# A transformer block whose planner leaves GpSimd only the norms' inverse roots, with fixed buffers and a new plan

## The chip, the core and the metric

The kernel runs on one core of one Trainium2 chip. The metric is the time of one launch in microseconds of device time, taken as the median of several runs. Lower is better.

## What is computed

Two layers of a diffusion transformer block work on 512 latent tokens and 256 context tokens of width 1024, all in float32. In each layer three token mixers read the same normalised and modulated input and their outputs are joined before one output projection; then follows a gated feed-forward network (FFN).

```
for l in range(2):
    u  = modulate(rmsnorm(h),  shift, scale)   @ w_in[l]     # latent tokens
    uc = modulate(rmsnorm(hc), cshift, cscale) @ w_in[l]     # context tokens
    na  = neighborhood_attention(q, k, v, k_ctx, v_ctx, rpb) # 6 heads of 64, windows of 8 x 16
    mla = latent_attention(...)                              # 6 heads, low-rank q and kv, rope
    lru = gelu(lg) * (scan_forward + scan_backward)          # gated linear recurrence
    h  = h + g_m * (concat(na, mla, lru) @ w_out[l])
    h  = h + g_f * (silu(y @ w_gate) * (y @ w_up)) @ w_down,  y = modulate(rmsnorm(h))
    # the context tokens go the same way in layer 0 alone
```

The shifts, scales and gates come from a product of a condition vector with `ada_w` (1024 x 6144 for each layer).

## The kernel before, in words

Activations lie transposed: 128 channels on the partitions, tokens along the free dimension (768 in layer 0, 512 for most of layer 1). Each float32 matrix product runs on TensorE as three products of a high and a low part: `split` (a copy to the type fp32r for the high part, tile `whi` for weights and `s` for operands, then a subtraction for the low part, `wlo` or `s`). So each weight tile that comes by DMA (tile `wst`) costs a cast and a subtraction of 128 x 1024 on some engine before TensorE can use it. The FFN's two first products use Strassen's scheme of seven products for 2 x 2 blocks: sums and differences of weight blocks (`weights`, written into `wst`) and of the operand's blocks (`operands`, tiles `lo`, `tmp`, `s`), then sums of the products (`Side.all`, `together`).

A norm's inverse root is made in `rstd`: a few columns of sums of squares go through TensorE, are scaled on VectorE into a tile `rn` (line 561), raised to the power -0.5 on GpSimd (line 697, "a root" below), and spread over the tokens by transposes on TensorE (line 524).

No engine order is written by hand. Every operation is recorded as an `Op` with a cost for each engine that could run it (`t` TensorE, `v` VectorE, `s` ScalarE, `g` GpSimd, `d` DMA issue). `Order.place` is a list planner: it takes the operation that can start first by its own model of the clocks, ranks and buffers, puts it on the engine that it thinks best, and gives out the program in that order. The roots name GpSimd alone; copies, casts, sums, differences and memsets name two or three engines, so the planner chose GpSimd for 276 of them. Its model holds one more thing: VectorE operations that are marked `both` (no operand in PSUM) and GpSimd operations exclude each other on a port. An operation on one side that would start while the other side is busy was moved to that one's end when candidates were compared.

The order in which the mixer's steps are recorded, and a lead for each in rank, stand in a table of text (`PLAN`, `LEAD`), one list for each layer. Steps are named by what they do (`lru_*`, `latent_*`, `near_*`, `out_part k` for the split of the k-th operand of the output projection). The output projection itself (tiles `A<-s,whi` at a mixer's end) and the FFN are recorded after them, and the planner may place their instructions among the last steps.

Tiles of one tag share a number of buffers (`BUFS`, for instance 15 of `s`, 4 each of `wst`, `whi` and `wlo`). The planner's model took the buffer that came free first; the framework then picked which one in fact.

## Time and profile before

| | us |
|---|---|
| three runs | 1832.73, 1825.57, 1832.43 (median 1832.43) |
| the profiled execution, its own time | 1837.95 |
| span of the profiled execution | 1835.4 |
| TensorE (PE) busy | 1720.5 |
| VectorE (DVE) busy | 1340.2 |
| ScalarE (ACT) busy | 770.2 |
| GpSimd (POOL) busy | 407.5 |

PE is the time of matmuls, PEld that of weight loads beside them. The mean granted clock of TensorE is 0.975 of full speed. The stages by the trace: start to 46 us; mixer of layer 0 with its output projection to about 506; change to the FFN (norm, `operands`) to 552; FFN of layer 0 to 1058; the norm between the layers to 1104; mixer of layer 1 to 1426; its change to the FFN to 1518; FFN of layer 1 to the end. In the views an instruction is given by the line of its helper: L518 a matmul, L524 a transpose, L544 and L546 a copy or cast on ACT and on DVE, L548 the same on POOL, L554 a sum or difference on DVE or POOL, L588 a multiply-add on DVE, L697 a root.

### The profile page before, as it was taken

What the parts mean: (1) busy time and instruction counts of PE and PEld (TensorE: products, weight loads), DVE (VectorE), ACT (ScalarE), POOL (GpSimd) and SP (SyncE); (2) the same over time, 40 slices, a digit from 0 to 9 for tenths busy, and PEclk for the clock granted to TensorE, in tenths of its full rate; (3) what the DMA queues carried; (4) which work ended last, traced back from release to release, by engine and by line L of the source; (5) the groups of instructions that cost most, each with busy time, mean ns of one, the idle gap of its engine ahead of it and who ended that gap; (6) DMA issues with size and microseconds to landing.
All of it is one profiled execution on the core that took longest, in us unless ns stands there. A gap on an engine that the chain in (4) does not pass through costs nothing.

```text
span 1835.4 us, 27989 instructions
## 1 busy us (share of the span) xinstructions
PE 1720.5 (94%) x10616; PEld 1472.5 (80%) x10616; DVE 1340.2 (73%) x2361; ACT 770.2 (42%) x1382; POOL 407.5 (22%) x326
## 2 busy tenths in 40 slices
PE   8989999999979999999999989998889989999998
PEld 4877665767959898989899968776678788898897
DVE  6574356766498888877879677576686797788776
ACT  5282245664153343323223233744565343343343
POOL 0142133233072121210111022213243240001010
PEclk9999899999989999999999989999999989999999
DMA  8121123233012334243434141212011123323332
GB/s 336 58 74 62 39 69 104 78 116 127 29 35 90 105 98 129 81 141 112 151 125 138 61 142 47 65 58 72 24 38 30 35 65 108 104 93 98 98 104 92
DMA packets 90998, 166.66 MB, mean 91 GB/s; under 512 B 10480, under 2 KB 53872, under 8 KB 90864
## 3 DMA queue, kind: packets, MB, share of 16 engines
q1 hardware_dynamic: 90864, 164.88, 28.1%
q8 instruction: 83, 1.36, 0.3%
q14 instruction: 51, 0.42, 0.1%
HBM read 160.65 MB, written 4.19 MB: 90 GB/s over the span
## 4 chain that ended last, share of the span: by engine, by line
PE 64%; DVE 22%; DMA 5%; issue 4%; ACT 3%; POOL 2%; SPq 0%; DVEq 0%; ACTq 0%; POOLq 0%
PE A L518 36%; PE B L518 22%; DVE wlo L554 6%; PE B L524 5%; DVE tmp L554 3%; DMA ast<-in_ada_dram 3%; DVE s L554 3%; DVE wst L554 2%; DMA wst<-in_wg_dram 1%; DVE acc L588 1%; POOL rn L697 1%; DVE s L546 1%; DVE lo L588 1%; DVE lo L554 1%; DVE hr L588 1%
## 5 line engine op out<-in xcount | busy, mean ns | idle before, releaser
L518 PE MATMUL A<-s,whi 128*128 128x256 f32 (+2 forms) x2192 | 546.9, 341 | 17.6 <-ACT s L544 5.5
L518 PE MATMUL B<-s,whi 128*128 128x384 f32 (+2 forms) x2032 | 465.9, 323 | 17.8 <-ACT hr L544 4.3
L518 PEld LDWEIGHTS A<-s,whi 128*128 128x128 f32 x2192 | 375.5, 190 | 72.2 <-ACT s L544 7.4
L544 ACT CAST whi<-wst 128x1024 fp32r<-128x1024 f32 (+2 forms) x281 | 227.0, 817 | 439.9 <-PE A L518 225.8
L518 PEld LDWEIGHTS B<-s,whi 128*128 128x128 f32 x2032 | 347.6, 193 | 32.2 <-ACT hr L544 4.6
L518 PE MATMUL A<-s,wlo 128*128 128x256 f32 (+2 forms) x1064 | 345.7, 338 | 1.2 <-DVE wlo L554 1.2
L554 DVE TENSOR_TENSOR wlo<-wst,whi 128x1024 fp32r<-128x1024 f32 (+3 forms) x303 | 319.9, 1066 | 12.1 <-ACT whi L544 8.4
L518 PE MATMUL B<-s,wlo 128*128 128x384 f32 (+2 forms) x1016 | 301.9, 320 | 0.2 <-DVE wlo L554 0.2
L518 PE MATMUL A<-lo,whi 128*128 128x512 f32 (+1 forms) x776 | 216.7, 358 | 4.7 <-DVE hr L588 1.8
L518 PEld LDWEIGHTS A<-s,wlo 128*128 128x128 f32 x1064 | 197.4, 191 | 15.8 <-DVE wlo L554 2.0
L518 PEld LDWEIGHTS B<-s,wlo 128*128 128x128 f32 x1016 | 190.6, 193 | 3.4 <-DVE wlo L554 0.5
L697 POOL TENSOR_TENSOR rn<-rn,con 128x12 f32<-128x12 f32 (+5 forms) x44 | 84.6, 1925 | 445.0 <-DVE rn L561 437.8
L518 PEld LDWEIGHTS A<-lo,whi 128*128 128x128 f32 x776 | 136.6, 188 | 31.7 <-issue 3.3
L588 DVE SCALAR_TENSOR_TENSOR hr<-A,mod,hr 128x512 f32<-128x512 f32 (+1 forms) x153 | 100.6, 659 | 60.2 <-PE A L518 60.1
L554 POOL TENSOR_TENSOR wst<-wst,wst 128x512 f32<-128x512 f32 x35 | 54.3, 1553 | 371.2 <-DVE wst L554 328.1
L518 PE MATMUL A<-lo,wlo 128*128 128x512 f32 (+1 forms) x388 | 136.2, 356 | 0.0
L518 PE MATMUL A<-s,s 128*128 128x512 f32 (+1 forms) x508 | 120.5, 354 | 14.2 <-ACT lo L533 4.5
L518 PEld LDWEIGHTS A<-s,s 128*128 128x128 f32 x508 | 81.2, 194 | 36.5 <-ACT lo L533 10.1
L546 DVE CAST whi<-wst 128x1024 fp32r<-128x1024 f32 (+3 forms) x45 | 32.7, 727 | 101.1 <-PE A L518 82.0
L588 DVE SCALAR_TENSOR_TENSOR acc<-ast,cc,acc 128x256 f32<-128x256 f32 x168 | 88.5, 527 | 19.2 <-DMA ast<-in_ada_dram 17.8
L554 POOL TENSOR_TENSOR wlo<-wst,whi 128x512 fp32r<-128x512 f32 (+3 forms) x25 | 40.9, 1637 | 262.2 <-ACT whi L544 260.9
L518 PE MATMUL B<-s,s 128*64 128x256 f32 (+2 forms) x720 | 87.5, 347 | 0.7 <-DVE sm L1411 0.5
(206 smaller groups left out, 2371.4 us busy)
## 6 DMA issues: line engine op xcount, KB each, us to landing
ast<-in_ada_dram SPq DMA_DIRECT2D x320, 128.0 KB, 2.2
wst<-in_wg_dram SPq DMA_DIRECT2D x44, 512.0 KB, 3.5
wst<-in_wu_dram SPq DMA_DIRECT2D x44, 512.0 KB, 3.5
wst<-in_wd_dram SPq DMA_DIRECT2D x80, 256.0 KB, 2.7
wst<-in_win_dram SPq DMA_DIRECT2D x32, 512.0 KB, 3.7
wst<-in_wout_dram SPq DMA_DIRECT2D x16, 512.0 KB, 3.7
hr<-in_x_dram SPq DMA_DIRECT2D x16, 384.0 KB, 3.6
s<-in_ada_dram SPq DMA_DIRECT2D x8, 768.0 KB, 11.5
```

Source lines behind the costliest of these rows:

```text
L518: od.add({"t": c}, lambda e: nc.tensor.matmul(ap(out), lhsT=ap(lhsT), rhs=ap(rhs), start=start, stop=stop, skip_group_check=more), [out], ...
L524: od.add({"t": 109.0}, lambda e: nc.tensor.transpose(ap(out), ap(in_), ap(ident)), [out], [in_, ident])
L544: nc.scalar.copy(out=ap(out), in_=ap(in_))
L546: nc.vector.tensor_copy(ap(out), ap(in_))
L554: (nc.vector if e == "v" else nc.gpsimd).tensor_tensor(out=ap(out), in0=ap(a), in1=ap(b), op=op)
L588: lambda e: nc.vector.scalar_tensor_tensor(out=ap(out), in0=ap(a), scalar=ap(s), in1=ap(b), op0=op0, op1=op1),
L697: lambda e: nc.gpsimd.tensor_tensor(out=ap(r[:, :w]), in0=ap(r[:, :w]), in1=ap(C("mhalf", 0, w)), op=ALU.pow),
```

## The change

With `alone` set, which it is from the start and everywhere, `Order.add` strikes GpSimd from every operation that another engine could run too. The planner's model of the port now lets an operation start while the other side holds the port and adds the rest of that time to its cost. A tile of a tag with several buffers is bound to the buffer that the model chose, as a tag of its own. The table of step orders and leads is another one for both layers.

```diff
-    latent_kv @-53, lru_out 1 @-1529, lru_in 0, lru_in 1 @20, near_v 1 @990, near_q 1, lru_gates 0 @695,
+    lru_start @-375, near_v 1 @-623, lru_in 0 @-182, latent_kv @1409, lru_gates 0 @-699, lru_in 1, near_q 1 @-27,
...
     def tile(self):
         if self.real is None:
-            self.real = self.pool.tile(list(self.shape), self.dt, tag=self.tag, name=f"{self.tag}_{self.id}",
-                                       bufs=self.bufs)
+            tag = self.tag if self.bufs == 1 else f"{self.tag}_{self.slot}"
+            self.real = self.pool.tile(list(self.shape), self.dt, tag=tag, name=f"{self.tag}_{self.id}", bufs=1)
...
-        self.line, self.free, self.loose = [], [0.0] * bufs, 0
+        self.line, self.free, self.loose = [], [(0.0, i) for i in range(bufs)], 0
...
+        if self.alone and len(cost) > 1:
+            cost = {e: c for e, c in cost.items() if e != "g"}
...
-                    if e == "g" or e == "v" and op.both:
-                        a, b = port["v" if e == "g" else "g"]
-                        if a <= st < b:
-                            st = b
...
+                    if e == "g" or e == "v" and op.both:
+                        a, b = port["v" if e == "g" else "g"]
+                        if a <= top[3] < b:
+                            fin_here += b - top[3]
...
             if e == "g" or e == "v" and op.both:
+                a, b = port["v" if e == "g" else "g"]
+                if a <= st < b:
+                    cost += b - st
                 port[e] = (st, st + cost)
...
-                    tg.free.append(b.end)
+                    tg.free.append((b.end, b.slot))
```

In the program GpSimd's list falls from 331 instructions to 55: 44 roots and what the start needs. DVE has 218 more, ACT 58 more and two loads of function tables; TensorE and the DMA queue have as many as before.

**The norm between the layers.** POOL before, up to the first root of layer 1 (`rn_10484`); the `wlo` and `whi` rows prepare weights of layer 1.

```order
L554 TENSOR_TENSOR tmp_10299<-tmp_10299,tmp_10404 128x512
L548 TENSOR_SCALAR whi_10438<-wst_10360 128x1024
L554 TENSOR_TENSOR wlo_10452<-wst_10313,whi_10426 128x1024
L554 TENSOR_TENSOR wlo_10478<-wst_10418,whi_10468 128x1024
L697 TENSOR_TENSOR rn_10484<-rn_10484,con_82 128x4
```

POOL now, at the same place; the two roots of 128x3 are those of the norm ahead of the FFN of layer 0.

```order
L704 TENSOR_TENSOR rn_5083<-rn_5083,con_84 128x3
L704 TENSOR_TENSOR rn_5098<-rn_5098,con_84 128x3
L704 TENSOR_TENSOR rn_10482<-rn_10482,con_84 128x4
L704 TENSOR_TENSOR rn_10541<-rn_10541,con_84 128x2
L704 TENSOR_TENSOR rn_10829<-rn_10829,con_84 128x6
```

Nothing stands between the roots any more.

DVE at that place, before: the scaling that the root waits for is the row `rn`, what follows the root is the row with `amix`.

```order
L546 CAST whi_10468<-wst_10418 128x1024
L554 TENSOR_TENSOR tmp_10454<-tmp_10454,tmp_10457 128x256
L561 TENSOR_SCALAR rn_10484<-B_10459 128x4
L554 TENSOR_TENSOR wlo_10486<-wst_10360,whi_10438 128x1024
L554 TENSOR_TENSOR tmp_10454<-tmp_10454,tmp_10461 128x256
```

DVE now:

```order
L553 CAST whi_10462<-wst_10417 128x1024
L561 TENSOR_TENSOR tmp_10449<-tmp_10449,tmp_10455 128x256
L561 TENSOR_TENSOR wlo_10475<-wst_10313,whi_10425 128x1024
L568 TENSOR_SCALAR rn_10482<-B_10458 128x4
L561 TENSOR_TENSOR tmp_10449<-tmp_10449,tmp_10460 128x256
L561 TENSOR_TENSOR wlo_10488<-wst_10361,whi_10452 128x1024
```

A subtraction of a weight tile that was POOL's (of `wst_10313`) stands ahead of the scaling on DVE.

**The end of the mixer of layer 1.** PE before: `ident,tmp` rows are the transposes of a near step's weights after the exponential, `A_13442<-s,whi` and `<-s,wlo` the output projection.

```order
L524 MATMUL B_13433<-ident_65,tmp_13397 128x128 x4
L518 MATMUL A_13442<-s_2584_13247,whi_11865 128x512
L524 MATMUL B_13446<-ident_65,tmp_13406 128x128 x4
L518 MATMUL A_13442<-s_2584_13247,whi_11865 128x512
L518 MATMUL B_13454<-s_2499_12887,s_2497_12882 128x256 x4
L524 MATMUL B_13459<-ident_65,tmp_13417 128x128 x4
L518 MATMUL A_13442<-s_2584_13247,wlo_11906 128x512
```

PE now, the last near step:

```order
L531 MATMUL B_13451<-ident_65,tmp_13377 128x128 x4
L531 MATMUL B_13458<-ident_65,tmp_13423 128x128 x4
L531 MATMUL B_13468<-ident_65,tmp_13435 128x128 x4
L531 MATMUL B_13480<-ident_65,tmp_13443 128x128 x4
L531 MATMUL B_13489<-ident_65,rb_13470 128x128
L531 MATMUL B_13489<-ident_65,rb_13478 128x128
L525 MATMUL B_13489<-s_2638_13465,s_2500_12961 64x256
```

Nine more rows of the last near step's product with the values follow, and then the output projection begins. Its matmuls stood among the last near steps before (96 of them in layer 0, 36 in layer 1) and start behind them now, in both layers.

## Rows read from the trace of the kernel before

**Rows 1.** The page's chain of work that ended last: shares of the span by engine.

```profile
PE 64%; DVE 22%; DMA 5%; issue 4%; ACT 3%; POOL 2%; SPq 0%; DVEq 0%; ACTq 0%; POOLq 0%
```

**Rows 2.** Stages: stretch, length, busy us (instructions) by engine; granted clock, DMA share, GB/s.

```profile
46.00:506.00 460.00, 437.29 (x2845) 341.15 (x2844) 273.64 (x550) 206.22 (x414) 125.28 (x97) 0.99 0.24 75
506.00:552.00 46.00, 31.19 (x153) 26.09 (x151) 43.47 (x62) 26.24 (x48) 34.90 (x26) 0.85 0.11 35
552.00:1058.00 506.00, 488.93 (x2772) 460.30 (x2773) 410.40 (x703) 162.21 (x252) 75.58 (x55) 0.99 0.36 112
1058.00:1104.00 46.00, 36.90 (x200) 30.74 (x199) 36.76 (x61) 19.12 (x37) 12.93 (x8) 0.85 0.42 139
1104.00:1426.00 322.00, 297.00 (x1878) 239.43 (x1878) 224.24 (x393) 169.41 (x313) 100.23 (x81) 0.97 0.16 49
1426.00:1518.00 92.00, 82.31 (x553) 75.99 (x552) 75.84 (x123) 42.56 (x83) 31.07 (x31) 0.89 0.17 52
1518.00:1836.00 318.00, 308.25 (x2034) 279.05 (x2034) 243.92 (x373) 121.43 (x199) 25.07 (x21) 1.00 0.31 98
sum 1836.00, PE 1720.55 PEld 1472.48 DVE 1340.18 ACT 770.16 POOL 407.48; mean PE 215.07 PEld 184.06 DVE 167.52 ACT 96.27 POOL 50.93
```

**Rows 3.** Page's groups, roots on POOL: count | busy us, mean ns | idle before, releaser.

```profile
L697 POOL TENSOR_TENSOR rn<-rn,con 128x12 f32<-128x12 f32 (+5 forms) x44 | 84.6, 1925 | 445.0 <-DVE rn L561 437.8
```

**Rows 4.** Groups by form, whole span: the same weight sums on POOL and on DVE.

```profile
L554 POOL TENSOR_TENSOR wst<-wst,wst 128x512 f32<-128x512 f32 x35 | 54.3, 1553 | 371.2 <-DVE wst L554 328.1 <-DVE wlo L554 16.5 <-DMA ast<-in_ada_dram 14.8
...
L554 DVE TENSOR_TENSOR wlo<-wst,whi 128x1024 fp32r<-128x1024 f32 x175 | 228.4, 1318 | 10.3 <-ACT whi L544 7.9
...
L554 DVE TENSOR_TENSOR wst<-wst,wst 128x512 f32<-128x512 f32 x97 | 83.1, 866 | 0.6
```

**Rows 5.** Groups by form on DVE from 460 to 506 us, where POOL does nothing.

```profile
L554 DVE TENSOR_TENSOR wlo<-wst,whi 128x1024 fp32r<-128x1024 f32 x4 | 4.9, 1220 | 0.2 <-ACT whi L544 0.2
...
L554 DVE TENSOR_TENSOR wst<-wst,wst 128x512 f32<-128x512 f32 x3 | 2.1, 689 | 0.1
```

**Rows 6.** Timeline (start us, us, what): DVE beside two roots, then beside POOL's differences.

```profile
510.62 2.27 POOL L697 TENSOR_TENSOR rn<-rn,con 128x3 f32<-128x3 f32 x2 [74.56 <-DVE rn L561]
510.66 0.68 DVE L554 TENSOR_TENSOR wst<-wst 128x512 f32<-128x512 f32 x1
...
527.01 0.55 DVE L554 TENSOR_TENSOR tmp<-lo,tmp 128x384 f32<-128x384 f32 x1
...
534.88 1.26 POOL L554 TENSOR_TENSOR lo<-lo,tmp 128x384 f32<-128x384 f32 x1 [0.96 <-DVE tmp L554]
535.20 1.36 DVE L554 TENSOR_TENSOR lo<-lo,tmp 128x384 f32<-128x384 f32 x1
```

**Rows 7.** Timeline at the norm between the layers; in brackets idle time and its releaser.

```profile
1090.75 3.31 POOL L554 TENSOR_TENSOR wlo<-wst,whi 128x1024 fp32r<-128x1024 f32 x1 [0.97 <-DVE rn L561]
...
1094.03 1.19 POOL L697 TENSOR_TENSOR rn<-rn,con 128x4 f32<-128x4 f32 x1
...
1095.27 1.12 PE L524 MATMUL B<-ident,rn 128*128 128x128 f32 x4 [6.21 <-POOL rn L697]
```

**Rows 8.** What PE waited for from 506 to 552 us: total us, times, longest.

```profile
PE B L518 <- POOL s L548: 1.7, 1, 1.7
PE A L518 <- POOL s L548: 1.6, 1, 1.6
```

**Rows 9.** Timeline of PE at the end of the mixer of layer 1.

```profile
1401.87 0.48 PE L518 MATMUL A<-s,whi 128*128 128x512 f32 x1
1402.19 0.60 PE L524 MATMUL B<-ident,tmp 128*128 128x128 f32 x4
...
1408.23 0.62 PE L518 MATMUL A<-s,whi 128*128 128x512 f32 x2
1408.69 0.40 PE L518 MATMUL A<-s,wlo 128*128 128x512 f32 x1
1408.93 0.62 PE L518 MATMUL A<-s,whi 128*128 128x512 f32 x2
...
1409.72 3.75 PE L518 MATMUL B<-s,s 128*64 128x256 f32 x48
```

**Rows 10.** Groups by form on ACT, whole span: a near step's exponential.

```profile
L533 ACT ACTIVATE tmp<-tmp,sm 128x512 f32<-128x512 f32 x48 | 34.4, 718 | 9.7 <-DVE sm L1411 9.5
```

More of the change, by code (lines that the diff above doesn't have):

```diff
@@ new lines @@
+    latent_query 3, latent_k 2 @-565, latent_job 0 0 @2223, latent_query 4 @-1458, latent_put 1 @-459,
+    latent_job 1 2 @688, latent_job 1 0 @1636, latent_query 5 @-568, near_bias 0 @-272, latent_job 1 1 @-149,
+    latent_put 2, near_job 0 0 @-24, near_job 0 1 @638, near_ctx 0 @-1250, near_prep 2 @1314, latent_job 2 0,
+    out_part 3 @-660, near_bias 2 @42, out_part 1 @-1265, latent_job 2 2, out_part 0 @566, latent_job 2 1,
+    near_prep 1 @-9, near_job 2 0, out_part 2 @1210, near_job 2 1 @-10, near_bias 1 @-1907, out_part 4 @1169,
@@ new lines @@
+    near_ctx 2, near_job 1 0 @-876, near_job 1 1 @1193, out_part 5 @-375, out_part 7 @222, near_ctx 1, out_part 6
+""", """
+    latent_kv @9, lru_in 0 @287, lru_in 1 @473, lru_gates 0 @495, near_k 2 @-261, near_k 0 @33, latent_k 0 @486,
+    lru_out 1 @906, lru_gates 1 @602, latent_rope @434, lru_out 0 @-1331, latent_keys @-657, near_v 0 @2500,
+    latent_q @1743, latent_k 1 @6, lru_start @-261, near_q 0 @971, near_q 1 @1945, near_k 1 @-7, latent_put 0 @1672,
+    latent_query 1 @-2, lru_scan 1 @1959, latent_query 0, latent_k 2 @-1209, near_q 2, lru_scan 0 @-200,
+    latent_v @-5, near_v 1 @-113, near_v 2 @339, near_prep 1 @872, latent_job 0 1 @15, latent_query 2,
+    latent_job 0 0, latent_query 3 @-2487, latent_put 1 @-24, out_part 1 @-71, latent_job 1 0 @-301,
+    latent_query 4 @-552, latent_query 5 @1987, latent_job 1 1 @88, latent_put 2, latent_job 2 1 @580,
+    near_bias 1 @800, near_job 1 0 @-540, near_job 1 1 @-163, near_prep 0 @83, latent_job 2 0, near_bias 0 @410,
+    near_prep 2 @-3, near_job 0 1 @1, near_bias 2, near_job 2 0 @-2500, near_job 2 1 @-5, out_part 6,
+    out_part 2 @2098, near_job 0 0 @248, out_part 3 @-1126, out_part 4 @2500, out_part 0 @-9, out_part 5 @-14,
+    out_part 7
@@ L242, in __init__ @@
         self.ops, self.bufs, self.tags = [], [], {}
-        self.shift, self.lead, self.gate = 0, 0, None
+        self.shift, self.lead, self.gate, self.alone = 0, 0, None, True
     def add(self, cost, emit, writes, reads, table=None, heat=1.0, middle=False, shape=0, both=False):
@@ L351, in place @@
                             break
-                        st = max(st, tg.free[j])
+                        st = max(st, tg.free[j][0])
                     if blocked:
                         continue
-                    if e == "g" or e == "v" and op.both:
-                        a, b = port["v" if e == "g" else "g"]
-                        if a <= st < b:
-                            st = b
                     if op.table is not None and e == "s" and table not in op.table:
@@ L394, in place @@
                     tg.line.remove(b)
-                tg.free.pop(0)
+                b.slot = tg.free.pop(0)[1]
             cost = op.cost[e]
@@ L878, in second @@
                 put(("T4", "T3"), j, pair(), 0, xs[4 + j][:, :n])
+        od.alone = True
         first()
         second()
+        od.alone = True
         return ops
@@ L1529, in activate @@
             return [one, two]
+        od.alone = True
         for h0, hn in GROUPS:
@@ L1545, in ffn @@
                             parts(n) if end and l < DEPTH - 1 else None)
+        od.alone = True
         return stats
```

25 lines of the change are left out of this document (4 added, 21 removed).

## The prediction

> **What bounds the kernel now.** I read the chain of waits first. It lies on TensorE for 64% and on VectorE for 22% of the span; GpSimd holds 2% [rows 1]. Then the stages: of a span of 1835.4 us the matmuls fill 1720.6, which leaves 115 us in which PE is idle [rows 2]. In the two FFN stages PE idles 17 us of 506 and 10 of 318; there only the matmuls themselves set the time. PE idles most, for its length, where operands for the next stage are made: 14.8 of 46 us from 506 to 552, 9.1 of 46 from 1058 to 1104, 9.7 of 92 from 1426 to 1518 [rows 2]. In these three stretches POOL is busy for 76, 28 and 34% of the time, and the granted clock falls to 0.85, 0.85 and 0.89: PE spent part of them at 1.2 GHz after it had stood still. The two mixers leave 23 and 25 us of idle PE, spread over many small waits.
>
> So the question is how much of what PE waits for goes through GpSimd, or through a VectorE that is held up by it, and what the other engines pay for taking its work.
>
> **What leaves POOL, and its price elsewhere.** POOL is busy for 407.5 us [rows 2], of which the 44 roots take 84.6 [rows 3]; they stay. The other 322.9 us go, spread over 276 instructions and a few at the start. The program has 218 of them more on DVE and 58 more on ACT. The commonest one, a sum of weight blocks of 128x512, takes 1553 ns on POOL [rows 4] and 689 ns on DVE when POOL is silent [rows 5], a factor of 0.44. The whole of POOL's work is thus 0.44 x 323 = 142 us on the faster engines, about 112 of it on DVE by the share of instructions and 30 on ACT.
>
> **What DVE gets back.** The same sum costs DVE 866 ns on average over the span [rows 4] against 689 ns with POOL silent [rows 5]: 97 x 177 ns = 17 us. The subtraction for a weight's low part costs 1318 against 1220 ns [rows 4, 5]: 175 x 98 ns = 17 us. Single rows show why: a difference of 128x384 takes 0.55 us alone, and 1.36 us when it starts inside a POOL difference, ending just after POOL's [rows 6]. These two groups give 34 us; the others of that kind must give some too, so 34 is a lower bound, and POOL's whole 323 us the upper one. DVE then has 1340 - 34 + 112 = 1418 us of work at most, 77% of the span: not a new bound on its own. In the FFN of layer 0, DVE's fullest long stage, it does 410 us in 506 and would get 0.44 x 75.6 = 33 us from POOL [rows 2], while most of the 34 us come back there and in the other FFN, since weight sums exist in FFNs alone. I cost the FFN stages' load at nothing on that ground; without that cover DVE would be at 88% there.
>
> **Do the roots still hold DVE up?** Beside two roots that run for 2.27 us, a DVE instruction of 128x512 took 0.68 us [rows 6], which is what it takes with POOL silent [rows 5]. The roots that stay cost DVE nothing. The Trainium skill, SBUF — State Buffer, section on who interferes with whom, has GpSimd take the shared port pair for a whole instruction and block a VectorE instruction with two SBUF inputs; the differences in the rows agree (0.55 to 1.36 us), the roots do not. By that rule the roots would keep their 84.6/407.5 = 21% of the lock-outs, and the 34 us freed would be 27; I go by the row.
>
> **The path, in terms.** The sum is made against the profiled execution's own 1837.95 us (its span of 1835.4 and 2.5 around it), which lies 5.5 us above the median of the runs.
> 1. POOL's own pieces on the chain: 2% of the span in all, 1% or a little more of it roots, so about 14 us of other work [rows 1, 3]. On another engine they take 0.44 of that: -8 us. Two places show it. At the norm between the layers the root waits behind a weight subtraction on POOL of 3.31 us, and PE for 6.21 us [rows 7]; with POOL's list empty ahead of the root 3.3 us go, and the new order gives back 1.2 us [rows 5], since DVE now does one of these subtractions ahead of the scaling that the root needs. From 506 to 552 PE waits directly on POOL casts for 3.3 us [rows 8]. Bounds: -14 and 0.
> 2. DVE's stalls on the chain: 34 us freed, and 22% of the span is 404 us of DVE's 1340 on the chain, three tenths [rows 1, 2]. That is -10 us. Bounds: 0, if the stalls lie off the chain, and -34.
> 3. The added 112 us on DVE and 30 on ACT: what of them replaces POOL's pieces is in term 1. The rest was off the chain on POOL and must stay off it on a busier engine. Bounds 0 and three tenths, +43 us. I take 0, nearest to the FFN row where DVE's load hardly changes, and keep the other end for the range.
> 4. The ends of the mixers. Before, the output projection's matmuls fill PE between the transposes of the last near steps [rows 9]; now they follow. In a near step a tile's exponential takes 0.72 us on ACT [rows 10], four transposes 0.60 us on PE and the products with the values 3.75 us for two steps [rows 9]. One step's chain from scores to values, exposed once, is the exponential, a copy out of PSUM that I cost like it, and the transposes: about 2 us, in two layers +4 us. Bounds: 0, and the whole cover, 36 matmuls in layer 1 and 96 in layer 0: three of 512 columns follow each other in 0.70 us, 1408.23 to 1408.93 [rows 9], so 132 of them take 31 us at most.
> 5. The new step orders within the mixers. Nothing in the rows prices an order. PE's idle time there is 23 + 25 us [rows 2]; an order can remove some of it, or add as much again. I take 0 and let the range hold half of it either way.
> 6. Buffers bound by the model, and the model's port: 0. Neither adds an instruction, and the tags' buffers were taken in turn already. A wait for a buffer that was free earlier elsewhere is at most an instruction's length here and there.
>
> Sum: -8 - 10 + 0 + 4 + 0 = -14 us, so 1824 for the profiled execution, and against the median 1832.4 - 14 = **1818 us**. A stall that goes uncovers the next: at 1095 the root itself and PE's transposes, from 506 to 552 DVE, which is busy for 43.5 of 46 us there [rows 2].
>
> **Rivals.**
> - *More: the stalls stood on the chain.* Contended DVE instructions are long because they are late for somebody; if all 34 us of term 2 were on the chain instead of a third, the time is 1818 - 24 = 1794 us. For it: the three stretches where PE starves are where POOL is busiest. Against: FFNs, with most weight sums, leave PE 27 us in all.
> - *No change.* The work that leaves POOL joins DVE's single queue; terms 1 and 2 are paid back by a third to a half of term 3 (+18 us of 43). The time is 1832 + 4 = 1836, or a little less, 1831. For it: PE is busy 94% and the freed time was mostly beside matmuls. Against: the direct waits [rows 7, 8].
> - *Slower: the near steps queue on DVE.* In the mixers POOL did 125.3 + 100.2 us, of which at most all 84.6 are roots; of the other 141 us 62 go to DVE and ACT [rows 2, 3], with little contention to win back. If half of it stands in front of copies and scalings that PE waits for, the mixers lose 31 us, the ends 4, and terms 1 and 2 give 18: 1832 + 17 = 1849; with two fifths, 1843. It decides from a quarter of the 62 us on, where the 14 us are used up. For it: PE already waits in the mixers for small things one after the other. Against: DVE is idle there for 40 and 30% of the time [rows 2].
> - That the change doesn't do what it says is out: the order shows 55 instructions on POOL.
>
> **How the numbers follow.** Forecast 0.40 (1808 to 1823), more 0.12 (below that), no change 0.30, slower 0.18. A measurement of this kernel can tell about 0.5%, 9 us, from no change: faster than 1823 has 0.52, within 1823 to 1842 0.30, slower 0.18. The range of 8 in 10 runs from the greater gain to the slower rival's two fifths: 1795 to 1845.
>
> **What would show it.** POOL's busy time near 85 us; the weight sum on DVE near 690 ns and the weight subtraction near 1220 ns everywhere; DVE near 1340 - 34 + 112 = 1418 us or less, the less the more was freed; ACT near 800. Between the layers the root starts right after its scaling and PE's 6.2 us shrink to about 3; from 506 to 552 PE's idle time falls by some 3 to 5 us. At the mixers' ends a wait of PE of some 2 us shows in the near steps' transposes or products. The prediction is wrong if the mixers' idle PE time grows by more than 15 us, or if DVE instructions stay long beside the roots.

## The result, and the profile after

The changed kernel takes **1778.29 us** (median of four runs, 1774.84 to 1781.88) against 1831.5 for the kernel before beside it (1825.57 to 1832.73): a ratio of 0.9716, 95% interval 0.9686 to 0.9746. That is faster by 53 us. Faster by over 0.5% was the likeliest side; the size was not: 14 us were forecast, and the time lies 17 us under the low end of the range. The profiled execution took 1774.84 us, which is 3.4 under its median, where that of before lay 5.5 over its own: the two traces are 62.7 us apart, of which about 9 are chance.

The page of the changed kernel, span and busy time by engine; the helpers' lines are seven higher than before (L525 a matmul, L531 a transpose, L551 a cast on ACT, L561 a sum or difference on DVE, L595 a multiply-add, L704 a root):

```profile
span 1772.7 us, 27751 instructions
PE 1694.2 (96%) x10616; PEld 1455.8 (82%) x10616; DVE 1326.4 (75%) x2579; ACT 812.8 (46%) x1442; POOL 88.7 (5%) x50
```

and its chain of work that ended last, by engine:

```profile
PE 80%; DVE 9%; ACT 5%; DMA 2%; POOL 2%; issue 1%; SPq 0%; ACTq 0%; DVEq 0%; POOLq 0%
```

VectorE took over 218 instructions and is busy for 14 us less than before; its share of the chain fell from 22 to 9% [rows 1]. The groups by form on DVE say how it got time back (count | busy us, mean ns):

```profile
L561 DVE TENSOR_TENSOR wlo<-wst,whi 128x1024 fp32r<-128x1024 f32 x180 | 217.7, 1223 | 11.4 <-ACT whi L551 8.7 <-PE A L525 0.5
L561 DVE TENSOR_TENSOR wst<-wst,wst 128x512 f32<-128x512 f32 x132 | 87.4, 687 | 0.5
L561 DVE TENSOR_TENSOR wlo<-wst,whi 128x512 fp32r<-128x512 f32 x124 | 84.5, 686 | 1.2 <-ACT whi L551 0.7
L595 DVE SCALAR_TENSOR_TENSOR acc<-ast,cc,acc 128x256 f32<-128x256 f32 x168 | 80.9, 483 | 18.4 <-DMA ast<-in_ada_dram 15.3 <-ACT acc L582 1.8
```

The weight sum went from 866 to 687 ns and the weight subtraction from 1318 to 1223 [rows 4], to what rows 5 show with GpSimd silent.

To see where the time went, both programs are cut at the same matmuls by their number in PE's order, so that each stage does as many products, in the FFNs the same ones. The windows of before, cut so (columns as in rows 2: mixer of layer 0, its change to the FFN, FFN, norm between the layers, and mixer, change and FFN of layer 1):

```profile
39.70:507.10 467.40, 444.69 (x2887) 346.40 (x2887) 280.72 (x566) 210.14 (x420) 125.28 (x97) 0.99 0.24 75
507.10:559.50 52.40, 35.95 (x172) 30.84 (x171) 48.12 (x67) 28.75 (x50) 36.34 (x27) 0.84 0.13 40
559.50:1059.90 500.40, 484.97 (x2758) 456.34 (x2757) 405.43 (x696) 159.46 (x250) 74.15 (x54) 1.00 0.36 112
1059.90:1119.90 60.00, 50.90 (x285) 42.83 (x284) 49.59 (x86) 28.25 (x51) 12.93 (x8) 0.89 0.35 115
1119.90:1439.80 319.90, 294.90 (x1866) 237.63 (x1865) 220.19 (x378) 162.17 (x301) 101.52 (x82) 0.97 0.16 50
1439.80:1500.30 60.50, 51.52 (x338) 47.52 (x337) 51.32 (x84) 31.75 (x64) 28.90 (x30) 0.83 0.14 45
1500.30:1830.10 329.80, 323.68 (x2161) 294.39 (x2161) 257.69 (x397) 130.35 (x215) 25.95 (x22) 1.00 0.31 97
```

and of the changed kernel:

```profile
38.80:506.60 467.80, 442.53 (x2888) 345.67 (x2883) 295.12 (x629) 225.90 (x434) 43.63 (x18) 1.00 0.24 76
506.60:552.50 45.90, 36.84 (x178) 29.50 (x172) 42.50 (x86) 27.65 (x54) 2.65 (x2) 0.81 0.14 46
552.50:1029.70 477.20, 476.00 (x2758) 452.52 (x2757) 391.99 (x739) 167.77 (x265) 0.00 (x0) 1.00 0.38 118
1029.70:1089.10 59.40, 50.79 (x285) 42.45 (x284) 49.31 (x91) 28.69 (x52) 3.29 (x2) 0.91 0.35 112
1089.10:1392.30 303.20, 287.89 (x1865) 232.96 (x1864) 221.46 (x425) 180.95 (x324) 34.87 (x18) 0.99 0.17 53
1392.30:1449.30 57.00, 48.95 (x339) 44.28 (x338) 49.72 (x106) 33.13 (x67) 1.79 (x2) 0.88 0.14 47
1449.30:1767.40 318.10, 317.16 (x2162) 292.12 (x2161) 249.57 (x417) 129.73 (x214) 0.00 (x0) 1.00 0.32 101
```

What counts here are the lengths and, behind each, PE's busy time. The FFN of layer 0 shrank by 23.2 us, that of layer 1 by 11.7, the mixer of layer 1 by 16.7, the two changes to the FFN by 10; the mixer of layer 0 and the norm between the layers hardly moved. In the FFN of layer 0 the idle time of PE was 15.4 us and is 1.2, so the rest of the 23 came out of PE's *busy* time: the same 2758 matmuls count 485 us before and 476 after. In the FFN of layer 1 it is 324 and 317 us, with a granted clock of 1.00 in both. Busy PE is not PE at its peak. In the mixer of layer 1 PE's idle time fell from 25.0 to 15.3 us and its busy time by 7, with the granted clock at 0.97 before and 0.99 after. PE's longest waits in the FFN of layer 0 before (total us, times, longest), by the view of waits from 560 to 1059 us:

```profile
PE B L518 <- DVE acc L588: 5.5, 5, 1.7
PE A L518 <- ACT s L544: 3.7, 4, 1.3
PE A L518 <- DVE tmp L554: 2.1, 4, 0.7
```

and all of them after, from 553 to 1029 us:

```profile
PE B L525 <- DVE acc L595: 0.7, 1, 0.7
PE A L525 <- DVE tmp L561: 0.5, 1, 0.5
```

### The profile page after: what moved, and what is told of

The parts are those of the page before. It is cut to its first block, busy times and chain, and to the rows that moved or that the text cites. A ratio compares the mean times of both kernels' runs of the same rounds, so it can differ in the third digit from the quotient of the medians.

```text
span 1772.7 us, 27751 instructions
## 1 busy us (share of the span) xinstructions
PE 1694.2 (96%) x10616; PEld 1455.8 (82%) x10616; DVE 1326.4 (75%) x2579; ACT 812.8 (46%) x1442; POOL 88.7 (5%) x50
## 4 chain that ended last, share of the span: by engine, by line
PE 80%; DVE 9%; ACT 5%; DMA 2%; POOL 2%; issue 1%; SPq 0%; ACTq 0%; DVEq 0%; POOLq 0%
PE A L525 45%; PE B L525 30%; PE B L531 4%; DVE s L561 2%; DMA ast<-in_ada_dram 2%; POOL rn L704 2%; DVE wlo L561 1%; ACT s L551 1%; ACT lo L540 1%; DVE tmp L561 1%; ACT s L540 1%; DVE lo L595 1%; DVE sm L614 1%; ACT tmp L540 1%; ACT tmp L551 1%
## 5 line engine op out<-in xcount | busy, mean ns | idle before, releaser
L525 PE MATMUL A<-s,whi 128*128 128x256 f32 (+2 forms) x2192 | 540.0, 339 | 10.4 <-ACT tmp L540 1.9
L525 PE MATMUL B<-s,whi 128*128 128x384 f32 (+2 forms) x2032 | 454.8, 319 | 10.8 <-ACT s L551 5.7
L551 ACT CAST whi<-wst 128x1024 fp32r<-128x1024 f32 (+3 forms) x291 | 237.4, 827 | 416.0 <-PE A L525 232.7
L525 PEld LDWEIGHTS A<-s,whi 128*128 128x128 f32 x2192 | 374.8, 190 | 62.7 <-ACT s L540 4.9
L525 PEld LDWEIGHTS B<-s,whi 128*128 128x128 f32 x2032 | 342.6, 191 | 23.9 <-ACT s L551 8.1
L525 PE MATMUL A<-s,wlo 128*128 128x256 f32 (+2 forms) x1064 | 341.6, 335 | 0.0
L561 DVE TENSOR_TENSOR wlo<-wst,whi 128x1024 fp32r<-128x1024 f32 (+2 forms) x328 | 314.7, 969 | 14.3 <-ACT whi L551 10.8
L525 PE MATMUL B<-s,wlo 128*128 128x384 f32 (+2 forms) x1016 | 296.1, 318 | 0.1
L525 PE MATMUL A<-lo,whi 128*128 128x512 f32 (+1 forms) x776 | 217.1, 359 | 1.3 <-ACT lo L551 1.3
L525 PEld LDWEIGHTS A<-s,wlo 128*128 128x128 f32 x1064 | 196.5, 190 | 14.5 <-DVE wlo L561 1.4
L525 PEld LDWEIGHTS B<-s,wlo 128*128 128x128 f32 x1016 | 187.2, 191 | 3.1 <-DVE wlo L561 0.7
L525 PEld LDWEIGHTS A<-lo,whi 128*128 128x128 f32 x776 | 136.9, 188 | 26.3 <-DVE hr L595 2.1
L704 POOL TENSOR_TENSOR rn<-rn,con 128x12 f32<-128x12 f32 (+5 forms) x44 | 87.9, 2000 | 1319.8 <-DVE rn L568 1312.6
L595 DVE SCALAR_TENSOR_TENSOR hr<-A,mod,hr 128x512 f32<-128x512 f32 (+1 forms) x153 | 100.9, 660 | 53.1 <-PE A L525 53.0
L525 PE MATMUL A<-lo,wlo 128*128 128x512 f32 (+1 forms) x388 | 136.9, 358 | 0.0
L525 PE MATMUL A<-s,s 128*128 128x512 f32 (+1 forms) x508 | 121.3, 352 | 11.1 <-ACT lo L540 5.5
L525 PEld LDWEIGHTS A<-s,s 128*128 128x128 f32 x508 | 80.8, 189 | 33.3 <-ACT lo L540 11.0
L553 DVE CAST whi<-wst 128x1024 fp32r<-128x1024 f32 (+3 forms) x39 | 25.4, 651 | 93.6 <-PE A L525 88.7
L595 DVE SCALAR_TENSOR_TENSOR acc<-ast,cc,acc 128x256 f32<-128x256 f32 x168 | 80.9, 483 | 18.4 <-DMA ast<-in_ada_dram 15.3
L525 PE MATMUL B<-s,s 128*64 128x256 f32 (+2 forms) x720 | 91.4, 347 | 0.1
L561 DVE TENSOR_TENSOR wst<-wst,wst 128x512 f32<-128x512 f32 x132 | 87.4, 687 | 0.5
L531 PE MATMUL B<-ident,tmp 128*128 128x128 f32 (+1 forms) x424 | 67.4, 276 | 17.4 <-ACT tmp L551 8.6
## 6 DMA issues: line engine op xcount, KB each, us to landing
s<-in_ada_dram SPq DMA_DIRECT2D x8, 768.0 KB, 11.6
```

Of the source, the lines that this page charges most:

```text
L525: od.add({"t": c}, lambda e: nc.tensor.matmul(ap(out), lhsT=ap(lhsT), rhs=ap(rhs), start=start, stop=stop, skip_group_check=more), [out], ...
L531: od.add({"t": 109.0}, lambda e: nc.tensor.transpose(ap(out), ap(in_), ap(ident)), [out], [in_, ident])
L551: nc.scalar.copy(out=ap(out), in_=ap(in_))
L553: nc.vector.tensor_copy(ap(out), ap(in_))
L561: (nc.vector if e == "v" else nc.gpsimd).tensor_tensor(out=ap(out), in0=ap(a), in1=ap(b), op=op)
L595: lambda e: nc.vector.scalar_tensor_tensor(out=ap(out), in0=ap(a), scalar=ap(s), in1=ap(b), op0=op0, op1=op1),
```

## The experiments

The stages of every kernel, cut at the same matmuls, as differences to the profiled execution of before in us (op: the change to the FFN). Executions of one kernel differ by up to 11 us in all, those of before by up to 16.

| kernel | mixer 0 | op 0 | FFN 0 | norm | mixer 1 | op 1 | FFN 1 | ratio to before, 95% interval |
|---|---|---|---|---|---|---|---|---|
| changed kernel | +0.4 | -6.5 | -23.2 | -0.7 | -16.6 | -3.5 | -11.7 | 0.9716 [0.9686, 0.9746] |
| e1_sub_dve | +6.4 | -4.5 | -9.1 | -1.6 | +2.8 | -2.7 | -8.9 | 0.9924 [0.9898, 0.9950] |
| e13_casts_to_act | -0.1 | -5.0 | -10.5 | -1.2 | +1.3 | -3.9 | -8.8 | 0.9897 [0.9875, 0.9919] |
| e2_replan_alone | +74.4 | -8.0 | -21.2 | -0.6 | +18.1 | -3.0 | -10.4 | 1.0308 [1.0265, 1.0351] |
| e5_ffn_alone | -2.3 | -8.2 | -21.7 | -0.1 | -0.6 | -0.1 | -10.4 | 0.9787 [0.9751, 0.9822] |
| e8_old_table | +50.2 | -8.2 | -24.7 | +4.8 | +17.6 | -2.6 | -13.0 | 1.0184 [1.0152, 1.0216] |
| e3_pool_allowed | +28.5 | -0.9 | +0.6 | -0.5 | -2.3 | -1.8 | -1.8 | 1.0162 [1.0126, 1.0197] |
| e7_old_port | +24.5 | -7.2 | -21.9 | -0.4 | -9.3 | -2.7 | -10.7 | 0.9865 [0.9831, 0.9898] |
| e15_no_port_model | +17.1 | -5.6 | -23.2 | +4.5 | +0.1 | -1.8 | -11.6 | 0.9909 [0.9886, 0.9932] |
| e4_pool_beside | +1.9 | -3.0 | -15.1 | -1.5 | -16.7 | +2.0 | -0.2 | 0.9851 [0.9815, 0.9888] |
| e9_memset_beside | +0.4 | -3.0 | -22.2 | -1.2 | -16.8 | +1.4 | -12.1 | 0.9750 [0.9725, 0.9774] |
| e14_copies_beside | -1.3 | -5.7 | -23.4 | -0.4 | -16.5 | -0.3 | -9.0 | 0.9754 [0.9726, 0.9782] |
| e6_free_buffers | -0.9 | -5.8 | -20.3 | 0.0 | -15.7 | -2.0 | -10.4 | 0.9748 [0.9717, 0.9780] |
| e11_after_again | +2.1 | -4.5 | -22.4 | -1.1 | -16.4 | -1.3 | -11.7 | 0.9726 [0.9698, 0.9754] |
| e12_free_again | -0.4 | -5.9 | -20.8 | -1.9 | -14.8 | -1.0 | -10.3 | 0.9773 [0.9744, 0.9801] |
| e10_dve_beside | -1.6 | -5.4 | -4.5 | -0.9 | -15.0 | +0.1 | +6.4 | 0.9936 [0.9914, 0.9957] |

**Taking GpSimd out without a new plan.** e1 keeps before's order to the last instruction and issues what the planner had put on GpSimd on VectorE:

```diff
-                op.emit(op.eng)
+                op.emit("v" if op.eng == "g" and len(op.cost) > 1 else op.eng)
```

> The plan, step table, model and buffers of the kernel before; only the 276 copies, sums, differences and memsets that its planner gave to GpSimd are issued by VectorE instead, at their places in the planned order. Theory A (GpSimd's work itself cost the time, by holding VectorE up on the port and by its own long instructions): the DVE weight sum falls from 866 to about 690 ns, and the time falls by most of the 53 us, to 1780 to 1800 us. Theory B (the new step table and the new model found a better order; the work on GpSimd was neutral): VectorE carries 112 us more and gets little back, 1825 to 1850 us.

It took 1819.06 us (before beside it 1834.95), between the ranges of both theories, so neither holds as it was put. The removal alone is worth 0.76%, 14 us; terms 1 to 3 of the prediction add up to 18, but it is spread otherwise than they say. The FFNs and their operands gain 25 us, the mixers lose 9. The other 38 us (0.9924 to 0.9716) come from placing the work anew, on VectorE and ScalarE, and from the buffers, whose part is below.

e13 sends the 58 casts and scalings among them to ScalarE:

```diff
-                op.emit(op.eng)
+                op.emit(("s" if "s" in op.cost else "v") if op.eng == "g" and len(op.cost) > 1 else op.eng)
```

> e1_sub_dve with one difference: of GpSimd's 276 instructions the 58 that ScalarE can do too (casts, scalings) go to ScalarE at their places, the other 218 to VectorE, as the changed kernel's engines have it; the order is that of before. It asks where the FFN of layer 0 gets the 14 us by which the changed kernel beats e1 there (-23 against -9). Theory B1 (the share of VectorE and ScalarE): the FFNs come near the changed kernel's, -18 or more in layer 0, and the time near 1805 us. Theory B2 (the new order of the work within the FFN): the FFN of layer 0 stays at -6 to -13 and the time within 6 us of e1's 1819.

1811.73 us. In the two FFNs VectorE is busy for 20 us less than before, and they are 19 us shorter. The FFN of layer 0 stays at -10.5, as theory B2 has it: not the split between the two engines but the new order gives most of the other 13 us there. e5 below, with a new order and the buffers of before, has 11 of them at the same VectorE time. The FFNs of layers 0 and 1 in e13, and the FFN of layer 0 in e5:

```profile
554.20:1043.90 489.70, 481.90 (x2757) 454.84 (x2756) 393.06 (x745) 161.76 (x255) 0.00 (x0) 1.00 0.37 115
1480.60:1801.50 320.90, 319.95 (x2161) 294.21 (x2160) 250.05 (x419) 129.83 (x214) 0.00 (x0) 1.00 0.32 100
```

```profile
549.80:1028.40 478.60, 477.62 (x2758) 455.52 (x2757) 392.47 (x738) 167.25 (x265) 0.00 (x0) 1.00 0.39 117
```

What in the new order does it, no run shows. e13's time is 7 us under e1's, a little outside B2's six, with ratios whose intervals meet; by the stages it lies in the mixer of layer 0.

**Placing it anew, with the old table of steps.** e2 is before with the rule alone:

```diff
+        if self.alone and len(cost) > 1:
+            cost = {e: c for e, c in cost.items() if e != "g"}
```

> The kernel before with the one rule added that strikes GpSimd from every operation that another engine can run; the old model of the port, the old step table and the framework's choice of buffers stay, the planner plans anew. Theory A: 1775 to 1795 us, with the FFN of layer 0 shorter by 20 us or more. Theory B: 1820 to 1840 us, the FFN of layer 0 within 5 us of its old 500 us.

e5 is e2 with the rule off but for `operands` and the FFN:

```diff
+        od.alone = True
         first()
         second()
+        od.alone = False
...
+        od.alone = True
         for h0, hn in GROUPS:
...
+        od.alone = False
```

> The kernel before with GpSimd struck from the operations of the FFNs, of their operands and of their down projections alone; the mixers keep GpSimd, and the old step table, model and buffers stay. By the stages of the runs so far the gain of 45 us in the FFNs and their operands comes from GpSimd's absence there, whatever the table (theory C), and the mixers' loss of 74 and 18 us in the second run from a table that was fitted to a plan with GpSimd. Theory C: the four FFN stages shorter by 38 to 48 us, the mixers within 8 us of before, 1785 to 1800 us. Rival D (the FFNs gained because of the new model of the port or what the planner inherits from the mixers): FFNs shorter by less than 20 us, 1810 to 1835 us.

e8 is the changed kernel with the table of before:

```diff
-    lru_start @-375, near_v 1 @-623, lru_in 0 @-182, latent_kv @1409, lru_gates 0 @-699, lru_in 1, near_q 1 @-27,
+    latent_kv @-53, lru_out 1 @-1529, lru_in 0, lru_in 1 @20, near_v 1 @990, near_q 1, lru_gates 0 @695,
...
```

> The changed kernel with the old table of step orders and leads. Theory C: the FFNs unchanged within 4 us; the mixers lose as in the second run, 60 to 110 us together, 1840 to 1890 us. Rival: the mixers' loss in the second run came from the old model of the port under the roots, not from the table; then the mixers here lose less than 25 us, under 1805 us.

e2 is slower than before, 1887.11 us, which misses both ranges; and yet its FFNs gain 21 and 10 us: the mixers pay 92. What PE waited for in e2's mixer of layer 0, with the window itself, is this:

```profile
40.40:582.20 541.80, 472.40 (x2886) 363.24 (x2886) 295.48 (x627) 225.20 (x438) 40.54 (x18) 0.94 0.21 65
```

```profile
PE B L520 <- DMA ast<-in_ada_dram: 22.5, 18, 2.3
PE B L526 <- ACT tmp L546: 11.7, 6, 5.7
PE A L520 <- ACT lo L535: 9.4, 14, 1.4
```

VectorE did as much there as in the changed kernel (295.5 against 295.1 us), but PE idles 69 us instead of 25: not load, but an order in which loads and small steps come late. PE's busy time is 30 us longer too (472.4 against 442.5), at a granted clock of 0.94 against 1.00. e5 leaves the mixers as they were and keeps the FFNs' gain: 1793.21 us. e8 shows the same with all of the change but its table: 1866.31 us, the mixers +68. So the FFNs gain the same with any table, and the new table is what turns the mixers' loss into a gain.

**The new table with another model.** e3 is the changed kernel with the rule off throughout:

```diff
-        self.shift, self.lead, self.gate, self.alone = 0, 0, None, True
+        self.shift, self.lead, self.gate, self.alone = 0, 0, None, False
...
-        od.alone = True
+        od.alone = False
...
```

> The changed kernel with GpSimd allowed again (new model of the port, new step table, fixed buffers). Theory A: the contended durations come back (the DVE weight sum near 860 ns) and with them 40 us or more: 1820 to 1840 us. Theory B: 1775 to 1795 us.

e15 has no port rule at all:

```diff
                     if e == "g" or e == "v" and op.both:
                         a, b = port["v" if e == "g" else "g"]
-                        if a <= top[3] < b:
-                            fin_here += b - top[3]
...
                 a, b = port["v" if e == "g" else "g"]
-                if a <= st < b:
-                    cost += b - st
```

> The changed kernel whose planner knows of no shared port at all, which is nearer to what the traces show of the roots, the only instructions left on GpSimd (no VectorE instruction was longer beside one). Theory C (the table of steps fits only the model it was found with): the mixers lose 10 to 40 us as with the old port model (e7_old_port), the FFN stages keep -20 and -10, and the time is 1785 to 1820. Rival (a truer model places better): 1778 us or less.

and e7 has, beside these two cuts, before's rule where candidates are compared:

```diff
+                    if e == "g" or e == "v" and op.both:
+                        a, b = port["v" if e == "g" else "g"]
+                        if a <= st < b:
+                            st = b
```

> The changed kernel with the old model of the port (an operation that would start while the other side is busy is moved to its end when candidates are compared, and its cost is not lengthened). With GpSimd left only the roots, the port enters the plan at 44 places, all in the mixers and norms. Theory C: the FFNs unchanged within 4 us; the mixers get a plan that the table was not fitted to, and lose 10 to 70 us. Rival: the model of the port matters little with so few roots, under 8 us in all.

1862.20 (over both ranges of e3), 1815.06 (e15) and 1808.62 us (e7). With GpSimd allowed again the FFNs' gain is gone (+0.6 and -1.8), with the new table too. With either other port rule the FFNs keep theirs, and the mixers are 33 (e15) and 31 us (e7) longer than in the changed kernel. The roots are the only work left on GpSimd, so all that the model of the port still does is to guess how long VectorE is held up beside a root. e15's guess, not at all, is the one that the traces bear out (the rows beside roots are in the next part), and it loses. That the table fits only the model of the changed kernel agrees with this, but isn't shown: no run has a table made for another model.

**What it is in GpSimd's work that costs the FFNs time.** Four kernels add work to the changed kernel at the same 88 places of the FFN stages, behind every second low-part subtraction of a pair of weight blocks. e4 adds three GpSimd subtractions:

```diff
+            for j in range(0, 3 * 160, 160):
+                nc.gpsimd.tensor_tensor(out=s, in0=s, in1=ap(lo[:, j : j + 176].f32()), op=ALU.subtract)
```

> The changed kernel, its plan untouched, with 264 GpSimd subtractions of 128x176 added in the FFNs: three after every second subtraction of a weight's low part, reading that tile into a scratch tile that nobody reads. They add no work to another engine; all they can do is hold VectorE up. In the FFNs of the kernel before 75 GpSimd instructions other than roots went with some 35 us more of FFN time. Theory A: 88 such groups of about 1.5 us lengthen VectorE's sums and differences beside them by half a microsecond or more each, and the FFN stages by 20 to 45 us: 1800 to 1825 us. Theory B, or if VectorE has slack in the FFNs: under 8 us, 1775 to 1786 us.

e9 adds a narrow one, which ties it to the place, and six memsets:

```diff
+            nc.gpsimd.tensor_tensor(out=s[:, :16], in0=s[:, :16], in1=ap(lo[:, :16].f32()), op=ALU.subtract)
+            for j in range(6):
+                nc.gpsimd.memset(s, 0.0)
```

> The changed kernel with, at the same 88 places of the FFN stages where e4_pool_beside put three GpSimd subtractions, one GpSimd subtraction of 128x16 and six GpSimd memsets of 128x176, which write and read nothing of SBUF; the output is the reference's. Theory A (VectorE is held up by GpSimd instructions that read two SBUF operands): only the 88 small subtractions can hold it up, the low-part subtractions stay near 686 ns (512 columns) and 1223 ns (1024), and the time stays at 1778 to 1785 us. Rival (any GpSimd work beside VectorE holds it up, or the issue of more instructions does): the time comes out near e4's 1805 us, with the low-part subtractions near 747 ns and VectorE's busy time up by some 35 us as there.

e14 adds three copies:

```diff
+            for j in range(0, 3 * 160, 160):
+                nc.gpsimd.tensor_scalar(out=s, in0=ap(lo[:, j : j + 176].f32()), scalar1=1.0, scalar2=1.0, op0=ALU.mult, op1=ALU.mult)
```

> The changed kernel with 264 GpSimd copies of 128x176, one SBUF operand read each, at the places where e4_pool_beside had 264 subtractions; the output is the reference's. Theory A (only instructions that read two SBUF operands hold VectorE up): like the memsets of e9_memset_beside, 1778 to 1787 us, the subtraction of a low part of 512 columns at 686 ns. Rival A3 (any read by GpSimd holds VectorE up; in the trace of before 4 of 29 VectorE differences beside GpSimd casts alone were long): between 1790 and 1805 us, that subtraction at 710 to 747 ns.

e10 adds two subtractions on VectorE itself:

```diff
+            for j in range(0, 2 * 160, 160):
+                nc.vector.tensor_tensor(out=s, in0=s, in1=ap(lo[:, j : j + 176].f32()), op=ALU.subtract)
```

> The changed kernel with two VectorE subtractions of 128x176 after the low-part subtraction at the same 88 places of the FFN stages; by the 128x512 subtraction's 686 ns one takes about 0.25 us, so VectorE gets some 40 to 45 us of work there, a little more than the 35 us by which e4's GpSimd work lengthened it. Theory A1 (VectorE's total time in the FFNs sets their length): the time grows by about the work added, to 1810 to 1823 us. Theory A2 (what costs is a single long stall in front of something that TensorE needs; evenly spread work is hidden): the time stays within 10 us of the changed kernel, 1778 to 1788. In between, the share that shows is read off, against e4's 27 us for 35.

e4 took 1805.05 us, and its groups on VectorE are long again:

```profile
L561 DVE TENSOR_TENSOR wst<-wst,wst 128x512 f32<-128x512 f32 x132 | 93.8, 735 | 0.5
L561 DVE TENSOR_TENSOR wlo<-wst,whi 128x512 fp32r<-128x512 f32 x124 | 92.1, 747 | 1.8 <-ACT whi L551 1.1
L595 DVE SCALAR_TENSOR_TENSOR acc<-ast,cc,acc 128x256 f32<-128x256 f32 x168 | 86.8, 518 | 15.1 <-DMA ast<-in_ada_dram 13.0 <-ACT acc L582 0.8
```

e9 took 1783.86 us, with an interval that meets that of the changed kernel on the same chip (0.9750 and 0.9726, below), with nearly as many microseconds of GpSimd in its FFNs as e4 (155 against 181). On VectorE and on GpSimd:

```profile
L561 DVE TENSOR_TENSOR wlo<-wst,whi 128x512 fp32r<-128x512 f32 x124 | 84.6, 687 | 1.9 <-ACT whi L551 1.3
```

```profile
L902 POOL MEMSET scr<- 128x176 f32 x528 | 130.2, 246 | 30.5
...
L900 POOL TENSOR_TENSOR scr<-scr,wlo 128x16 f32<-128x16 f32 x88 | 48.5, 551 | 970.5 <-DVE wlo L561 951.8 <-DVE rn L568 9.6 <-DVE acc L595 7.8
```

No lengthening (687 against 686 ns): GpSimd busy beside VectorE does not hold it up in itself, nor do 88 of its subtractions when they are 16 columns wide. The 4 us between e9 and the changed kernel are within the noise. e14's copies took 1786.56 us, and the same subtraction 702 ns:

```profile
L561 DVE TENSOR_TENSOR wlo<-wst,whi 128x512 fp32r<-128x512 f32 x124 | 86.5, 702 | 1.3 <-ACT whi L551 0.7
```

VectorE's busy time grew by 35 us with the subtractions (1326.4 to 1361.4) and by 7 with the copies (1333.6), for 207 and 146 us of GpSimd. The mean over the span hides what a copy does. The 25 subtractions of this form that lie beside a copy average 773 ns and the 99 others 684; in e4 the 37 beside a subtraction average 896 and the 87 others 683. One of e14's, which starts inside the copies:

```profile
1625.56 1.48 POOL L901 TENSOR_SCALAR scr<-wlo 128x176 f32<-128x176 f32 x3 [4.08 <-DVE wlo L561]
...
1626.77 0.81 DVE L561 TENSOR_TENSOR wlo<-wst,whi 128x512 fp32r<-128x512 f32 x1
```

So theory A is wrong in one point: copies, which read one operand, hold VectorE up too. They do it to fewer instructions and for a shorter time. Of the VectorE instructions with two operands outside PSUM, 67 are longer by over 40 ns beside copies (7 us in all) and 116 beside e4's subtractions (34 us). Instructions with an operand in PSUM are not held up: `tmp<-tmp,B` of 128x384 takes 547 and 543 ns beside the copies and the subtractions, 547 and 546 elsewhere. That the added reads cost by holding the `wlo` tiles longer is out: no engine waited for e4's subtractions, and for e14's copies one did, once, for 0.7 us. e14's interval includes both nothing and some 10 us, so its loss isn't settled.

e10 took 1818.74 us, 39 more than the changed kernel on the same chip (e11 below). The work it added:

```profile
L901 DVE TENSOR_TENSOR scr<-scr,wlo 128x176 f32<-128x176 f32 x176 | 60.2, 342 | 6.0
```

One took 342 ns where I had put 250, so it was 60 us, of which 39 show: 0.65 of each microsecond. The FFN of layer 0 in e10:

```profile
552.50:1048.40 495.90, 483.39 (x2758) 455.01 (x2758) 418.29 (x820) 168.36 (x265) 0.00 (x0) 0.99 0.37 113
```

In e4 it is 35 us of VectorE's time for 25 us (0.9851 against 0.9716), 0.71; the intervals allow about 0.45 to 0.95 there, and 0.55 to 0.75 in e10. So in these FFNs, where PE seems to idle for one microsecond, most of a microsecond more on VectorE shows in the time, whether it is work or waiting for a port. VectorE's total is not all: e13 and e5 have the same and differ by 11 us in the FFN of layer 0.

**Fixed buffers.** e6 and e12 are the changed kernel with the framework choosing among a tag's buffers again, e11 is the changed kernel beside e12:

```diff
-            tag = self.tag if self.bufs == 1 else f"{self.tag}_{self.slot}"
-            self.real = self.pool.tile(list(self.shape), self.dt, tag=tag, name=f"{self.tag}_{self.id}", bufs=1)
+            self.real = self.pool.tile(list(self.shape), self.dt, tag=self.tag, name=f"{self.tag}_{self.id}",
+                                       bufs=self.bufs)
```

> The changed kernel with the framework choosing buffers again; plan, model and table as changed. Theory C costs the buffers at nothing: 1772 to 1786 us. Rival: buffers that the model did not choose bring waits, above all in the mixers, where lifetimes differ: 10 us or more, 1788 us and up.

> The changed kernel as it is, beside e12_free_again on the same chip, to have their difference without a change of chip. Every theory: 1775 to 1782 us, a ratio of 0.969 to 0.975.

> The changed kernel with its tags' buffers picked by the framework again instead of the model, beside e11_after_again on the same chip. Prediction's term (fixed buffers are worth nothing): the two ratios agree within 0.3%. Rival (the model's plan holds better when the program takes the buffers that the model took): this one is 5 to 10 us slower, 0.3 to 0.6%, as the single comparison of e6_free_buffers suggested (1785.25 against 1778.29 us).

e6 1785.25 us, ratio 0.9748 [0.9717, 0.9780]; e11 1779.52, 0.9726 [0.9698, 0.9754]; e12 1790.76, 0.9773 [0.9744, 0.9801]. Both comparisons have the fixed buffers ahead, by 0.3 and 0.5%, and the intervals of e11 and e12 still touch (0.9754 and 0.9744): a gain of some 6 to 11 us is likely and not shown. The stages show 3 to 4 us of it in the FFNs: with fixed buffers they take 477.1 and 318.0 us (e11 477.9 and 318.0), with free ones 480.0 and 319.3 (e6) and 479.5 and 319.4 (e12).

None of these kernels was faster than the changed one.

## Why the prediction was right or wrong

**Terms 1 to 3, the work off GpSimd: -18 forecast, -14 measured (e1), -19 in e13.** The sum held; its parts did not. Where the prediction looked, at the norm and the operands, it was right in kind. At the norm the root starts right behind its scaling, and PE's wait shrank from 6.21 us [rows 7] to 3.76 in the profiled execution and to 2.79 in that of e11, the same kernel again; about 3 was forecast. The timelines of both:

```profile
1060.28 0.17 DVE L568 TENSOR_SCALAR rn<-B 128x4 f32<-128x4 f32 x1
...
1060.52 2.59 POOL L704 TENSOR_TENSOR rn<-rn,con 128x4 f32<-128x4 f32 x1 [548.39 <-DVE rn L568]
1060.68 1.23 DVE L561 TENSOR_TENSOR wlo<-wst,whi 128x1024 fp32r<-128x1024 f32 x1
...
1063.16 1.12 PE L531 MATMUL B<-ident,rn 128*128 128x128 f32 x4 [3.76 <-POOL rn L704]
```

```profile
1066.20 1.12 POOL L704 TENSOR_TENSOR rn<-rn,con 128x4 f32<-128x4 f32 x1 [551.23 <-DVE rn L568]
...
1067.38 1.11 PE L531 MATMUL B<-ident,rn 128*128 128x128 f32 x4 [2.79 <-POOL rn L704]
```

The root itself took 2.59 us in the first and 1.12 in the second, against 1.19 before, and the whole stage gained only 0.7 and 1.1. From operand to FFN in layer 0 PE's idle time fell from 16.4 to 9.1 us (length less busy time), more than the 3 to 5 foretold; POOL's casts are gone from its waits [rows 8], and ScalarE's are late next:

```profile
PE B L525 <- ACT s L551: 4.0, 3, 2.3
PE A L525 <- DVE s L561: 0.9, 1, 0.9
```

**Term 2's size.** 34 us of stalls were a lower bound. Five groups, by before's counts and means less after's (weight sums 866 and 687 ns, low parts of 1024 columns 1318 and 1223, of 512 columns 744 and 686, multiply-adds into `acc` 527 and 483, differences `wst<-wst` 831 and 689), make 97 x 0.179 + 175 x 0.095 + 107 x 0.058 + 168 x 0.044 + 41 x 0.142 = 53 us. Row by row it is more still: 491 VectorE instructions of before lie beside GpSimd's work other than roots, and they are together 123 us longer than the changed kernel's medians for the same forms. So DVE came to 1326 us and not to 1418, though by those medians the added instructions are 127 us and not 112. "Three tenths on the chain" was too little where it mattered: e4 and e10 price a microsecond of VectorE in the FFNs at 0.65 to 0.71, and in e13 the FFNs lose 19 us for 20.

**Term 3's ground is the first step that failed:** "PE idles 17 us of 506 and 10 of 318; there only the matmuls themselves set the time", on which the FFNs' load was costed at nothing. PE's idle time is no measure of how far a stage is from its floor. All of it went but about a microsecond in each, and 9 and 7 us of busy time with it (485 to 476, 324 to 317). e10 shows it best: where PE idled 1.2 us of 477, 26 more microseconds of VectorE (418.3 against 392.0) make the stage 18.7 longer, of which less than 12 are idle time of PE. VectorE's 88%, which the prediction worked out for that stage and passed over, was the number to price: it was 81% before and is 82% now, and at that share most of a microsecond more already shows. The chance for "more: the stalls stood on the chain" was put at 0.12 because the FFNs leave PE 27 us in all.

**Term 5 is the second, and the greater in us:** "Nothing in the rows prices an order", so it took 0, and half of PE's idle time either way for the range, in the mixers alone. The new placing, with the fixed buffers in it, is worth 38 us behind e1 and 33 behind e13, nearly the whole of the 39 us by which the forecast fell short. By the traces it is 25 us in the mixers and 17 in the FFNs behind e1 (1816.2 to 1772.7, 43.5 us), 17 and 16 behind e13 (1806.8 to 1772.7, 34.1 us); for the order in the FFNs the prediction named no term at all. In the mixers an order can lose far more than PE's idle time of 48 us: one rule, GpSimd struck out, costs 92 us with the old table (e2), and the new table wins 16 in the changed kernel, and loses 15 to 26 with another port rule or with GpSimd allowed (e7, e15, e3).

**Term 4, +4 for the mixers' ends: not seen.** From 430 to 507 us PE idles 0.2 us of 77, and from 1320 to 1393 3.1 of 73. In the second stretch transposes wait 2.2 us for ScalarE, and before they waited 3.5 us there for a copy on VectorE. **Term 6, 0 for fixed buffers and the port's model:** the buffers are worth 3 to 4 us in the FFNs and probably up to 11 in all; of the model nothing is known apart from its table.

**The roots: right.** They run as before:

```profile
L704 POOL TENSOR_TENSOR rn<-rn,con 128x12 f32<-128x12 f32 (+5 forms) x44 | 87.9, 2000 | 1319.8 <-DVE rn L568 1312.6 <-DVE sm L611 7.2
```

That VectorE's groups are at their lengths with GpSimd silent does not show it, since the FFNs, where most of them run, have no roots. The rows beside roots do: the subtraction of 128x1024 that starts inside the root of 2.59 us above takes 1.23 us. In the changed kernel 83 VectorE instructions lie beside roots, and none is over 8 ns longer than the median of its form; in before 66 lie beside roots alone, and they are no longer either. By the Trainium skill, SBUF — State Buffer, section Who interferes with whom, a VectorE instruction with two SBUF inputs contends with a GpSimd instruction that reads SBUF, and not with one that only writes it. The subtractions of e4, the copies of e14 and the memsets of e9 agree; the roots and the subtractions of 128x16 in e9 read SBUF and lengthen nothing, and there the measurement decides.

**The rivals.** The slower one (the near steps queue on DVE) is what e1 shows in small, +9 us in the mixers with all the work on VectorE; with the casts on ScalarE (e13) it is +1. What e2 shows in large is a program order that fits no longer; with the new table the mixers of the changed kernel escape it. "More" comes nearest, on the side of the result: the freed time of VectorE showed almost whole in the FFNs (e13). But 33 to 38 of the 53 us come from the placing and the buffers, which it doesn't name, so a time near its own would have been luck. "No change" fell with its premise that the freed time lay beside matmuls.

## What to carry to other kernels

PE busy for 97% of a stage does not say that PE sets its length: the same matmuls counted 324 us and, with the work placed otherwise, 317 at the same granted clock. Price the engine that feeds them, here VectorE at 81% of the stage, by adding a known amount of work to it and seeing what share of it shows. When a planner's engines, costs or orders change, split the change in two, the work moved at its old place and the work placed anew, and price the second too: here it was the larger, and of either sign by the table (e2, e8 and the changed kernel).

## What the runs showed of the hardware that was not expected

- GpSimd's memsets (528 of 128x176, 246 ns each) and its subtractions of 128x16 (88, 551 ns each) beside VectorE's subtractions lengthened none (687 ns against 686); subtractions of 128x176 lengthened the same form to 747 ns, copies of 128x176 to 702, as means over the whole span, and to 896 and 773 where they lay beside it.
- The same root of 128x4, with GpSimd idle for some 550 us ahead of it, took 2.59 us in one execution of the changed kernel and 1.12 us in another (e11).
- 207 us of GpSimd subtractions took 35 us from VectorE, and 25 us of the kernel's time, though nobody read what they made.
